# Interleaved rotary embedding on one core: the fp32 tail of the last row is tied to a later store

## The chip, the core and the metric

The kernel runs on one core of one Trainium2 chip. The metric is the device time of one execution in microseconds (us). Before the change it is 316.97 us, the median of three runs (316.95 to 317.14).

## What is computed

The input `x` has 8 batches (called rows here, 0 to 7) of 2048 positions, 16 heads and 64 elements, in fp32: 8.39 MB for each row. Neighbouring elements form pairs, and every pair is rotated by the angle of its position:

```python
x1, x2 = x_pairs[..., 0], x_pairs[..., 1]
out1 = x1 * cos - x2 * sin
out2 = x1 * sin + x2 * cos
out  = np.stack([out1, out2], axis=-1)     # fp32, interleaved again
```

`cos` and `sin` are 2048 x 32 in fp32 and are shared by rows and heads.

## The kernel before

**Layout.** The 2048 positions of a row are laid over 128 partitions, K = 16 positions in each. So a partition holds 16 x 1024 elements of a row, which are 64 KB of contiguous fp32 in memory and 32 KB of bf16 on the chip. The buffer `rows_sb` has NX = 5 slots of one row each, in bf16. Row b lives in slot b % 5: rows 5, 6 and 7 reuse slots 0, 1 and 2.

**Transfers.** `load` and `store` (lines 54 to 63) are DMAs issued by GpSimd (POOL). They convert between fp32 in memory and bf16 in `rows_sb` on the way, and they all go through one queue, called software_dynamic in the profile. A pair of rows goes in one DMA (lines 56 and 63), a single row or part of one in another (lines 54 and 61). Two pieces go another way, as plain fp32 DMAs issued by SyncE (SP), through the queue called hardware_dynamic: the first HEAD = 4 positions of each partition of row 0 (line 90, "the head"), which ScalarE (ACT) converts to bf16 at line 99, and the last TAIL = 4 positions of each partition of row 7 ("the tail"), which ACT converts to fp32 at line 131 and SP stores at line 132. Each of them is 2048 KB of fp32.

**Work.** `rotate` does three VectorE (DVE) operations for each row: the row times the signed sines into `qt` (line 79), the row times the cosines in place (line 80), and the sum with the pair-swapped `qt` (line 85).

**Order.** The schedule is written by hand (`tc.manual_schedule()`), so each engine runs its instructions in the order of the code. The waits between engines are put in from the tiles that instructions share: an instruction that writes a part of a tile waits for earlier readers and writers of that part, DMAs included. The kernel uses this for ordering alone at lines 112 and 130: a copy of a single element writes into a slot, and so has to wait for whatever still reads it.

The end of the order is what the change touches:

```python
store(3, 2)                    # L63: rows 3, 4 from slots 3, 4
rotate(5); rotate(6)
store(5, 2)                    # L63: rows 5, 6 from slots 0, 1
rotate(7)
store(7, k1=K - TAIL)          # L61: first 12 positions of row 7
...
nc.scalar.copy(out=rows_sb[:1, 4, 0, :1], in_=last[:1, K - 1, :1])   # L130
nc.scalar.copy(out=tail, in_=last[:, K - TAIL :])                    # L131
nc.sync.dma_start(out=out_t[:, B - 1, K - TAIL :], in_=tail)         # L132
```

(The three lines with `rotate` and `store` are set closer together here than in the file.) Line 130 reads row 7 and writes one element of slot 4, so it waits for the last rotation and for the store of rows 3 and 4. Lines 131 and 132 come behind it, on ACT and on SP. After the last instruction there is the closing sequence of the program, which the trace lists under line 158: SP waits for every DMA, and the engines meet at a barrier.

Of the kernel before, what the change touches and what calls it, by code (L numbers as in the profile page):

```python
# [2 lines left out]

# [4 lines left out]


@with_exitstack  # L10
def kernel(
    ctx: ExitStack,
    tc: tile.TileContext,
    x: bass.AP,
    cos: bass.AP,
    sin: bass.AP,
    out: bass.AP,
):
    nc = tc.nc
    fp32 = mybir.dt.float32  # L20
    bf16 = mybir.dt.bfloat16
    mult = mybir.AluOpType.mult
    add = mybir.AluOpType.add

    B, S, H, D = x.shape
    P = 128
    K = S // P
    D2 = D // 2
    HD = H * D
    NX = 5  # L30
    HEAD = 4
    TAIL = 4
    REST = 2

    x_t = x.rearrange("b (p k) h d -> p b k (h d)", p=P, k=K)
    out_t = out.rearrange("b (p k) h d -> p b k (h d)", p=P, k=K)
    cos_t = cos.rearrange("(p k) c -> p (k c)", p=P, k=K)
    sin_t = sin.rearrange("(p k) c -> p (k c)", p=P, k=K)

    consts = ctx.enter_context(tc.tile_pool(name="consts", bufs=1))  # L40
    stage = ctx.enter_context(tc.tile_pool(name="stage", bufs=1))

    cos_sb = consts.tile([P, K * D2], fp32)
    sin_sb = consts.tile([P, K * D2], fp32)
    c_tab = consts.tile([P, K, D], bf16)
    s_tab = consts.tile([P, K, D], bf16)
    mark = consts.tile([1, 1], bf16)

    rows_sb = consts.tile([P, NX, K, HD], bf16)

    def load(b, n=1, k0=0, k1=K):
        s = b % NX
        if n == 1:
            nc.gpsimd.dma_start(out=rows_sb[:, s, k0:k1], in_=x_t[:, b, k0:k1])  # L54
        else:
            nc.gpsimd.dma_start(out=rows_sb[:, s : s + n], in_=x_t[:, b : b + n])  # L56

    def store(b, n=1, k1=K):
        s = b % NX
        if n == 1:  # L60
            nc.gpsimd.dma_start(out=out_t[:, b, :k1], in_=rows_sb[:, s, :k1])  # L61
        else:
            nc.gpsimd.dma_start(out=out_t[:, b : b + n], in_=rows_sb[:, s : s + n])  # L63

    def rotate(b, k0=0, k1=K):

        nk = k1 - k0
        xp = rows_sb[:, b % NX, k0:k1]
        qt = stage.tile([P, K, HD], bf16, name="qt", tag="work")

        def rows(a):
            return a.rearrange("p k (h e) -> p k h e", h=H, e=D)

        def tab(a):
            return dataclasses.replace(
                a, offset=a.offset + k0 * D, ap=[a.ap[0], [D, nk], [0, H], [1, D]]
            )

        nc.vector.tensor_tensor(out=rows(qt[:, :nk]), in0=rows(xp), in1=tab(s_tab), op=mult)  # L79
        nc.vector.tensor_tensor(out=rows(xp), in0=rows(xp), in1=tab(c_tab), op=mult)  # L80
        q_swap = dataclasses.replace(
            qt, offset=qt.offset + 1, ap=[qt.ap[0], [2, nk * HD // 2], [-1, 2]]
        )
        x3 = xp.rearrange("p k (a j) -> p (k a) j", j=2)
        nc.vector.tensor_tensor(out=x3, in0=x3, in1=q_swap, op=add)  # L85
        return qt

    with tc.manual_schedule():
        head = stage.tile([P, HEAD, HD], fp32, name="st", tag="work")
        nc.sync.dma_start(out=head, in_=x_t[:, 0, :HEAD])  # L90
        load(0, k0=HEAD)
        nc.gpsimd.dma_start(out=cos_sb, in_=cos_t)  # L92
        nc.gpsimd.dma_start(out=sin_sb, in_=sin_t)  # L93
        load(1, 2)
        load(3)
        load(4, k1=K - REST)
        load(4, k0=K - REST)

        nc.scalar.copy(out=rows_sb[:, 0, :HEAD], in_=head)  # L99
        s2 = s_tab.rearrange("p k (i j) -> p (k i) j", j=2)  # L100
        nc.vector.tensor_copy(out=s2[:, :, 0], in_=sin_sb)  # L101
        nc.vector.tensor_scalar_mul(s2[:, :, 1], sin_sb, -1.0)  # L102
        nc.vector.tensor_copy(  # L103
            out=c_tab.rearrange("p k (i j) -> p (k i) j", j=2),
            in_=cos_sb.to_broadcast([P, K * D2, 2]),
        )
        rotate(0, 0, HEAD)
        rotate(0, HEAD, K)
        rotate(1)

        nc.scalar.copy(out=mark, in_=rows_sb[:1, 4, K - REST - 1, :1])  # L111
        nc.scalar.copy(out=rows_sb[:1, 0, 0, :1], in_=rows_sb[:1, 0, 0, :1])  # L112
        store(0, 2)
        rotate(2)
        store(2)
        load(5, 2)
        load(7)
        rotate(3)
        rotate(4)
        store(3, 2)  # L120
        rotate(5)
        rotate(6)
        store(5, 2)
        rotate(7)
        store(7, k1=K - TAIL)


        tail = stage.tile([P, TAIL, HD], fp32, name="st", tag="work")
        last = rows_sb[:, 7 % NX]
        nc.scalar.copy(out=rows_sb[:1, 4, 0, :1], in_=last[:1, K - 1, :1])  # L130
        nc.scalar.copy(out=tail, in_=last[:, K - TAIL :])  # L131
        nc.sync.dma_start(out=out_t[:, B - 1, K - TAIL :], in_=tail)  # L132


# [1 line left out]
_INS = ['x', 'cos', 'sin']  # L136
_OUTS = [((8, 2048, 16, 64), 'float32')]


# [23 lines left out]
```

## Time and profile before

| what | value |
|---|---|
| median of three runs | 316.97 us (316.95 to 317.14) |
| the profiled execution | 317.52 us |
| its span, first to last instruction | 315.7 us |
| DVE busy | 210.3 us (67%) |
| ACT busy / POOL busy | 8.9 us / 8.9 us |
| share of software_dynamic (POOL's queue) of 16 DMA engines' span | 96.6% |
| share of hardware_dynamic (SP's queue) | 5.7% |
| read from / written to HBM | 67.63 MB / 67.11 MB |

The profiled execution is 0.55 us above the median, and 1.8 us of its time lie outside the span. A DMA is cut into packets that 16 DMA engines work on. Here a packet is one partition's piece of a row. The trace records start, length, size and queue of each packet. For the store of a whole row every DMA engine has eight packets of 64 KB, and for the tail eight packets of 16 KB. At the end of each DMA every engine has one further packet of 4 bytes, its signal. A DMA has landed once all sixteen signals are in. All times below are on the scale of the page, from the start of the span.

### The profile page before, as it was taken

How to read it: one execution, taken by the hardware profiler on the slowest of the kernel's cores; microseconds unless marked ns; L12 is line 12 of the kernel's file. 1: busy time of each engine (PE TensorE's matmuls, PEld its weight loads, DVE VectorE, ACT ScalarE, POOL GpSimd, SP SyncE). 2: the span in 40 equal slices, each digit the busy share in tenths (PEclk: the TensorE clock that was granted, in tenths of full speed). 3: DMA queues.
4: the chain of work that ended last, by engine and by line, in shares of the span. 5: the costliest groups of instructions: out<-in, count | busy, mean ns of one | idle time of the engine just before them, and what ended most of it. 6: DMA issues, size and time to landing. Idle time of an engine off the chain costs nothing.

```text
span 315.7 us, 117 instructions
## 1 busy us (share of the span) xinstructions
DVE 210.3 (67%) x30; ACT 8.9 (3%) x6; POOL 8.9 (3%) x18
## 2 busy tenths in 40 slices
DVE  0009995099999999999992000899999999900000
ACT  1030000000000000000000000000000000040000
POOL 5000000000000000000000000000000000000000
DMA  8999999999999999999999999999999999999997
GB/s 260 254 282 199 199 199 266 199 199 220 220 232 257 399 531 399 399 498 432 399 199 253 212 199 199 266 199 332 440 490 399 399 506 423 399 399 465 459 372 299
DMA packets 2816, 102.24 MB, mean 324 GB/s; under 512 B 256, under 2 KB 256, under 8 KB 512
## 3 DMA queue, kind: packets, MB, share of 16 engines
q0 software_dynamic: 2528, 98.04, 96.6%
q1 hardware_dynamic: 288, 4.19, 5.7%
HBM read 67.63 MB, written 67.11 MB: 427 GB/s over the span
## 4 chain that ended last, share of the span: by engine, by line
DVE 66%; another core or an unknown queue 13%; ACTq 1%; issue 0%; ACT 0%; DVEq 0%
DVE rows_sb L80 22%; DVE rows_sb L85 22%; DVE qt L79 22%; ACTq L158 1%; DVE c_tab L103 0%; ACT rows_sb L130 0%; DVEq L79 0%; DVEq L80 0%
## 5 line engine op out<-in xcount | busy, mean ns | idle before, releaser
L79 DVE TENSOR_TENSOR qt<-rows_sb,s_tab 128x16384 bf16<-128x16384 bf16 (+2 forms) x9 | 69.7, 7743 | 42.0 <-DMA rows_sb<-in_x_dram 41.8
L80 DVE TENSOR_TENSOR rows_sb<-rows_sb,c_tab 128x16384 bf16<-128x16384 bf16 (+2 forms) x9 | 69.7, 7743 | 0.4
L85 DVE TENSOR_TENSOR rows_sb<-rows_sb,qt 128x16384 bf16<-128x16384 bf16 (+2 forms) x9 | 69.7, 7744 | 0.3
L101 DVE CAST s_tab<-sin_sb 128x512 bf16<-128x512 f32 x1 | 0.5, 454 | 23.8 <-DMA sin_sb<-in_sin_dram 23.8
L63 POOL DMA_DIRECT2D out_dram<-rows_sb x3 | 2.2, 719 | 184.0 <-ACT rows_sb L112 94.3
L130 ACT COPY rows_sb<-rows_sb 1x1 bf16<-1x1 bf16 x1 | 0.2, 194 | 177.5 <-DVE rows_sb L85 177.5
L99 ACT CAST rows_sb<-st 128x4096 bf16<-128x4096 f32 x1 | 3.6, 3604 | 13.2 <-DMA st<-in_x_dram 13.2
L131 ACT CAST st<-rows_sb 128x4096 f32<-128x4096 bf16 x1 | 3.6, 3598 | 0.0
L54 POOL DMA_DIRECT2D rows_sb<-in_x_dram x5 | 2.9, 605 | 19.1 <-DMA out_dram<-rows_sb 18.3
L111 ACT COPY mark<-rows_sb 1x1 bf16<-1x1 bf16 x1 | 0.2, 193 | 80.3 <-DMA rows_sb<-in_x_dram 80.3
L61 POOL DMA_DIRECT2D out_dram<-rows_sb x2 | 1.1, 556 | 40.4 <-DVE rows_sb L85 40.4
L56 POOL DMA_DIRECT2D rows_sb<-in_x_dram x2 | 1.5, 728 | 25.0 <-DMA out_dram<-rows_sb 25.0
L99 ACT ACT_TABLE_LOAD x1 | 1.3, 1283 | 0.7 <-PEq L147 0.7
L103 DVE CAST c_tab<-cos_sb 128x1024 bf16<-128x1024 f32 x1 | 0.7, 685 | 0.0
L93 POOL DMA_DIRECT2D sin_sb<-in_sin_dram x1 | 0.6, 562 | 0.0
L92 POOL DMA_DIRECT2D cos_sb<-in_cos_dram x1 | 0.6, 554 | 0.0
L102 DVE TENSOR_SCALAR s_tab<-sin_sb 128x512 bf16<-128x512 f32 x1 | 0.4, 444 | 0.0
L112 ACT COPY rows_sb<-rows_sb 1x1 bf16<-1x1 bf16 x1 | 0.2, 188 | 0.0
L147 POOL MEMSET const-float32-0.0<- 128x1 f32 x1 | 0.1, 99 | 0.2 <-issue 0.2
L147 POOL MEMSET const-bfloat16-1.0<- 128x1 bf16 x1 | 0.1, 103 | 0.0
L147 POOL MEMSET const-float32-1.0<- 128x1 f32 x1 | 0.1, 99 | 0.0
L147 POOL MEMSET const-uint8-127<- 128x1 uint8 x1 | 0.1, 99 | 0.0
## 6 DMA issues: line engine op xcount, KB each, us to landing
rows_sb<-in_x_dram POOLq DMA_DIRECT2D x2, 8192.0 KB, 58.5
rows_sb<-in_x_dram POOLq DMA_DIRECT2D x2, 4096.0 KB, 68.0
out_dram<-rows_sb POOLq DMA_DIRECT2D x1, 6144.0 KB, 37.3
rows_sb<-in_x_dram POOLq DMA_DIRECT2D x1, 3584.0 KB, 94.8
rows_sb<-in_x_dram POOLq DMA_DIRECT2D x1, 3072.0 KB, 21.2
st<-in_x_dram SPq DMA_DIRECT2D x1, 2048.0 KB, 14.4
out_dram<-st SPq DMA_DIRECT2D x1, 2048.0 KB, 33.7
rows_sb<-in_x_dram POOLq DMA_DIRECT2D x1, 512.0 KB, 96.8
```

What stands on the lines that cost most here:

```text
L54: nc.gpsimd.dma_start(out=rows_sb[:, s, k0:k1], in_=x_t[:, b, k0:k1])
L56: nc.gpsimd.dma_start(out=rows_sb[:, s : s + n], in_=x_t[:, b : b + n])
L61: nc.gpsimd.dma_start(out=out_t[:, b, :k1], in_=rows_sb[:, s, :k1])
L63: nc.gpsimd.dma_start(out=out_t[:, b : b + n], in_=rows_sb[:, s : s + n])
L79: nc.vector.tensor_tensor(out=rows(qt[:, :nk]), in0=rows(xp), in1=tab(s_tab), op=mult)
L80: nc.vector.tensor_tensor(out=rows(xp), in0=rows(xp), in1=tab(c_tab), op=mult)
L85: nc.vector.tensor_tensor(out=x3, in0=x3, in1=q_swap, op=add)
L92: nc.gpsimd.dma_start(out=cos_sb, in_=cos_t)
L99: nc.scalar.copy(out=rows_sb[:, 0, :HEAD], in_=head)
L103: nc.vector.tensor_copy(out=c_tab.rearrange("p k (i j) -> p (k i) j", j=2), in_=cos_sb.to_broadcast([P, K * D2, 2]),)
L131: nc.scalar.copy(out=tail, in_=last[:, K - TAIL :])
L158: with _tile.TileContext(nc) as tc:
```

## The change

The one-element copy at line 130 writes into slot 6 % 5 = 1 instead of slot 4. Slot 1 holds row 6, which is read by the store of rows 5 and 6. So line 130 now waits for that store (and for the last rotation, as before), and lines 131 and 132 come behind it. Nothing else changes: every engine has the same instructions in the same order. The waits of line 130 grow from three semaphores to five.

```diff
         tail = stage.tile([P, TAIL, HD], fp32, name="st", tag="work")
         last = rows_sb[:, 7 % NX]
-        nc.scalar.copy(out=rows_sb[:1, 4, 0, :1], in_=last[:1, K - 1, :1])
+        nc.scalar.copy(out=rows_sb[:1, 6 % NX, 0, :1], in_=last[:1, K - 1, :1])
         nc.scalar.copy(out=tail, in_=last[:, K - TAIL :])
         nc.sync.dma_start(out=out_t[:, B - 1, K - TAIL :], in_=tail)
```

## The prediction

> **What bounds the kernel now.** I read the page's slices and queues first, then its DMA issues.
>
> ```profile
> DVE  0009995099999999999992000899999999900000
> DMA  8999999999999999999999999999999999999997
> q0 software_dynamic: 2528, 98.04, 96.6%
> q1 hardware_dynamic: 288, 4.19, 5.7%
> out_dram<-rows_sb POOLq DMA_DIRECT2D x1, 6144.0 KB, 37.3
> out_dram<-st SPq DMA_DIRECT2D x1, 2048.0 KB, 33.7
> ```
>
> The DMA engines are busy from end to end, and DVE is idle in the last five slices. The bound is the DMA engines. The last two rows are the store of row 7 and the tail. From the timeline of the last part:
>
> ```profile
> 250.95 0.72 POOL L63 DMA_DIRECT2D out_dram<-rows_sb  x1 [82.44 <-DVE rows_sb L85]
> ...
> 276.86 0.19 ACT L130 COPY rows_sb<-rows_sb 1x1 bf16<-1x1 bf16 x1 [177.48 <-DVE rows_sb L85]
> 276.96 3.60 ACT L131 CAST st<-rows_sb 128x4096 f32<-128x4096 bf16 x1
> 277.13 0.54 POOL L61 DMA_DIRECT2D out_dram<-rows_sb  x1 [25.46 <-DVE rows_sb L85]
> 280.58 0.35 SPq L132 DMA_DIRECT2D out_dram<-st  x1
> ```
>
> Line 130 was released by the last rotation (L85). Its other wait, for the store of rows 3 and 4, was over by 256.2, when the last signal of that DMA came. So the old tie delays nothing. Adding the page's time to landing to the issue, row 7 lands at 277.13 + 37.3 = 314.43 and the tail at 280.58 + 33.7 = 314.28. Next, the DMA traffic between 286.7 and 296.3, and then the window table (stretch, length, busy DVE, ACT and POOL, clock, DMA share, GB/s):
>
> ```profile
> DMA packets 112, 4.19 MB, mean 437 GB/s; under 512 B 0, under 2 KB 0, under 8 KB 0
> q0 software_dynamic: 48, 3.15, 76.0%
> q1 hardware_dynamic: 64, 1.05, 26.8%
> ```
>
> ```profile
> 277.00:286.70 9.70, 0.00 (x0) 3.56 (x2) 0.54 (x1) 1.00 1.01 432
> 287.00:296.00 9.00, 0.00 (x0) 0.00 (x0) 0.00 (x0) 1.00 1.02 435
> 297.00:304.00 7.00, 0.00 (x0) 0.00 (x0) 0.00 (x0) 1.00 1.04 442
> 306.20:313.40 7.20, 0.00 (x0) 0.00 (x0) 0.00 (x0) 1.00 2.04 437
> ```
>
> In the first and last stretch data move only on POOL's queue, in the two between both queues take turns packet by packet. The rate is 432 to 442 GB/s either way. (The share of 2.04 in the last counts waiting signal packets as busy.) Last, the closing sequence, as the trace lists line 158, and SP's wait in it:
>
> ```profile
> L158 SPq EVENT_SEMAPHORE  x8: 17/28/28, 297.3 to 315.7; - x8
> L158 POOLq DRAIN  x3: 45/82/37927, 277.1 to 315.5; - x3
> ...
> SPq L158 <- DMA out_dram<-rows_sb: 33.4, 2, 17.1
> ```
>
> SP takes the DMAs in a fixed order: that of rows 5 and 6 (297.3), that of row 7 (314.43), four others that were over long ago, and last the tail. A POOL drain ends at 277.1 + 37.93 = 315.03.
>
> **Part 1: when the tail starts.** A 64 KB row takes 2.41 us on each DMA engine when POOL's queue runs alone (packet starts 279.55, 281.96, 284.37) and 3.03 us beside a tail packet (287.42, 290.45, 293.48). A tail packet costs 0.62 us. Four of them stood ahead of the landing of rows 5 and 6 at 297.30 (64 packets on q1 over 16 engines). The new wait puts them behind it, so that store lands at 297.30 - 4 x 0.62 = 294.8. ACT and SP need from 276.86 to 280.58, 3.72 us, and a further wait instruction some 0.05 us: SP issues the tail at about 298.6, 18 us later than now. Nothing is queued behind line 130 on ACT but line 131, and nothing behind line 132 on SP but the closing waits. POOL has issued the store of row 7 at 277.13 and waits for neither, DVE is done.
>
> **Part 2: where the DMA engines end.** With no tail before it, the store of row 7 starts at 294.1 on the first engine. Its eight 48 KB packets take 1.81 us each when alone (306.21, 308.02, 309.83, 311.64), so POOL's queue alone lasts until 308.5. The tail reaches the engines between 1.0 us after its issue (the head: issue 0.74, first packet 1.74) and 6.2 us (the tail before: 280.58 to 286.78, behind packets already taken in), so between 299.6 and 304.8. That is 3.7 to 8.9 us before POOL's queue is empty, and this is the cover of the 18 us delay: no engine goes idle, the same packets come in another order. If the tail were issued after 307.5, every further us would cost one. The end is 308.5 + 8 x 0.62 = 313.48 on the first engine, where it is 313.44 now, and 0.41 us later on the last one. Between three and eight tail packets now run alone at the very end. Alone such a packet took 0.61 us after the store of rows 5 and 6 (296.52 to 297.13), and in the head 0.62 us. Change of part 2: +0.04 us, from -0.1 to +0.2.
>
> **Part 3: the closing sequence.** Now row 7 signals last, the final signal arriving 0.56 us after its packet starts (313.85 to 314.41). SP sees it at 314.43 and steps through the remaining waits until 314.67, where it checks the tail. Afterwards row 7 signals first and those steps are done while the tail still runs. The tail's last signal packet starts at about 313.9 and arrives 0.34 to 0.43 us later (0.34 for the head, 0.43 for the store of rows 3 and 4): 314.25 to 314.35. SP passes its last wait at about 314.3 instead of 314.67, so 0.35 us earlier. Then POOL's drain: it ended at 315.03, 0.23 us after SP had reported at 314.80 and 0.62 us after row 7 had landed. No POOL instruction runs from 277.67 on, so I read it as waiting for POOL's own DMAs. If so, it will end some two us earlier, and the barrier opens 0.05 us after SP's report at 314.45: 314.50 instead of 315.07, a gain of 0.57 us. If it follows SP instead, only the 0.35 us. I take 0.5, nearer to the drain that waits for its DMAs.
>
> **Sum.** The profiled span ends 0.04 - 0.5, about 0.46 us earlier: 317.52 becomes 317.06 us, and the median of 316.97, which is 0.55 below the profiled execution, becomes 316.5.
>
> **One wait weighed.** The sixteen signal packets of the tail, started at 306.21 on the first engine, took 7.28 us each, against 22 ns for those of the head. On each engine they end with the signal of row 7: 306.21 + 7.28 = 313.49, and 313.44 + 0.05. I read this as a wait for the other queue's writes. [...] The trace agrees in the end times, but shows no SP store that ends alone.
>
> **Rivals.** (a) *The close shortens by more than I count.* If the drain goes, the landing delay falls to the head's 0.34 us, and the tail's packets at the end run at 0.61, the gain is 0.57 + 0.05 + 0.08 = 0.7: 316.3, to 316.1. For it: a drain of 37.93 us. Against: each piece is at its best end. (b) *The tail's signal has its own delay*, the case slower than before. If the 7.28 us belong to an SP store into memory and not to the other queue, they follow the last data and nothing hides them: tail done near 313.9 + 7.3 = 321.2, time 316.97 + 321.2 - 314.3 = 323.9. It decides from a signal wait of about 1.6 us, where the gain of the close is used up and 0.64 us are lost. For it: the only SP store in the trace shows this wait. Against: it ends to 0.05 us with the signal of row 7. (c) *Lone tail packets run slower.* The first packets of the head took 0.89 to 1.40 us; at 1.1 for five packets the loss is 5 x 0.48 = 2.4 us, less 0.5: 318.9. Against: the head's following packets and the lone tail packet at 0.61 to 0.62. (d) *Nothing moves*: the close keeps its length, since its pace is set by the drain and that by something else. 316.97 + 0.04 = 317.0. That the new tie does nothing is out: its store lands 18 us after the last rotation.
>
> **Chances.** A measurement of this kernel tells about 0.2% from no change, which is 0.63 us: 316.34 to 317.60 is no difference. My forecast (316.4 to 316.8) has 0.55, (d) 0.15, (a) 0.20, (b) 0.05, (c) 0.05. So faster 0.20, same 0.70, slower 0.10. The range takes in (a), the forecast and (d) with the 0.2 us of part 2: 316.1 to 317.3. It leaves out (b) and (c).
>
> **What would show it.** In the profile afterwards: SP's DMA of line 132 at 298.6; line 130 released by a DMA near 294.8; the first packet on SP's queue between 299.6 and 304.8; a GB/s line that stays near 435 until 313.9; tail signal packets with lengths far below 7 us; the tail landing at 314.3 and row 7 one to three us before it; POOL's drain ending before 314.5. Wrong would be: an idle stretch on the DMA engines after 308.5, lone tail packets well above 0.62 us, or a tail signal that waits.

## The result, and the profile after

The median fell from 316.98 us (22 runs) to 316.35 us (22 runs): 0.63 us less, ratio 0.9981, 95% interval 0.9975 to 0.9986. The forecast was 316.5 us, with 316.1 to 317.3 as its range. The gain lies at the very edge of what the prediction called no difference, and 0.05 us under the band that it called its own forecast (316.4 to 316.8).

The lines of the page after that answer to those shown before: slices and queues, then the last two DMAs with their us to landing.

```profile
DVE  0009995099999999999992000899999999910000
DMA  8999999999999999999999999999999999999997
q0 software_dynamic: 2528, 98.04, 96.8%
q1 hardware_dynamic: 288, 4.19, 3.4%
out_dram<-rows_sb POOLq DMA_DIRECT2D x1, 6144.0 KB, 34.0
out_dram<-st SPq DMA_DIRECT2D x1, 2048.0 KB, 15.5
```

The DMA engines are as full as before. The share of SP's queue fell from 5.7% to 3.4%, which is the waiting of its signal packets that has gone (7.28 us on each engine, 2.3% of the span, are now 9 ns). The timeline after:

```profile
276.48 0.55 POOL L61 DMA_DIRECT2D out_dram<-rows_sb  x1 [25.46 <-DVE rows_sb L85]
294.25 0.19 ACT L130 COPY rows_sb<-rows_sb 1x1 bf16<-1x1 bf16 x1 [195.42 <-DMA out_dram<-rows_sb]
294.35 3.60 ACT L131 CAST st<-rows_sb 128x4096 f32<-128x4096 bf16 x1
297.97 0.35 SPq L132 DMA_DIRECT2D out_dram<-st  x1
```

Line 130 is now released by a DMA, and SP issues the tail at 297.97 instead of 280.58. Row 7 lands at 276.48 + 34.0 = 310.5 and the tail at 297.97 + 15.5 = 313.5: the order of the two has turned round. Next, the closing sequence (line 158). The first of SP's drains comes 0.04 us behind its last wait, and the second one, 0.055 us later, is SP's report to the barrier (times of the report are its start). The barrier opens with the first of the four POOL semaphore instructions. Here are the lines of the kernel before:

```profile
L158 POOLq EVENT_SEMAPHORE  x4: 17/17/17, 315.1 to 315.6; - x4
L158 SPq DRAIN  x3: 7/7/7, 314.7 to 315.3; - x3
```

And of the changed kernel:

```profile
L158 SPq EVENT_SEMAPHORE  x8: 17/28/28, 298.4 to 314.3; - x8
L158 POOLq EVENT_SEMAPHORE  x4: 17/17/17, 313.7 to 314.2; - x4
L158 POOLq DRAIN  x3: 45/90/34653, 276.5 to 314.1; - x3
L158 SPq DRAIN  x3: 7/7/7, 313.6 to 313.9; - x3
```

Last, what SP waited for in it (us in total, times, longest us):

```profile
SPq L158 <- DMA out_dram<-rows_sb: 12.1, 1, 12.1
SPq L158 <- DMA out_dram<-st: 2.8, 1, 2.8
```

The last that SP waits for is now the tail, for 2.8 us. POOL's long drain ended at 276.454 + 34.653 = 311.11, well before that, and the barrier opened at 313.67, 0.03 us after SP's report at 313.64. Before, the drain ended at 315.03, after SP's report at 314.79, and the barrier opened at 315.07.

The profiled executions differ by more than the medians: 317.52 and 316.12 us. Of these 1.40 us, 0.69 were there when the store of rows 3 and 4 signalled (last signal packet at 255.813 before, 255.127 after), ahead of anything the change touches. This is a spread between executions: a kernel with the new tie, the last experiment below, has that packet at 255.91. So I count from it. From that packet to the end of the span it is 59.925 us before and 59.223 us after. The 0.70 us between them fall into three parts:

| us | before | after | difference |
|---|---|---|---|
| from that packet to the last signal packet of all | 58.04 | 58.03 | -0.01 |
| from the last signal packet to the last landing | 0.56 | 0.35 | -0.21 |
| from the last landing to the end of the span | 1.33 | 0.85 | -0.48 |

The DMA engines need the same time. The gain is in what follows them.

### The profile page after: what moved, and what is told of

Its sections match the earlier page's. It is cut to its first block, busy times and chain, and to the rows that moved or that the text cites. A ratio compares the mean times of both kernels' runs of the same rounds, so it can differ in the third digit from the quotient of the medians.

```text
span 314.4 us, 118 instructions
## 1 busy us (share of the span) xinstructions
DVE 210.3 (67%) x30; ACT 8.9 (3%) x6; POOL 8.9 (3%) x18
## 4 chain that ended last, share of the span: by engine, by line
DVE 42%; issue 17%; DMA 14%; another core or an unknown queue 13%; ACTq 1%; POOL 0%; ACT 0%; DVEq 0%; POOLq 0%
DMA out_dram<-rows_sb 14%; DVE rows_sb L80 14%; DVE rows_sb L85 14%; DVE qt L79 14%; ACTq L158 1%; POOL out_dram L63 0%; DVE c_tab L103 0%; ACT rows_sb L130 0%; ACTq L130 0%; DVEq L80 0%; DVEq L79 0%; POOLq L63 0%; POOLq L61 0%
## 6 DMA issues: line engine op xcount, KB each, us to landing
out_dram<-st SPq DMA_DIRECT2D x1, 2048.0 KB, 15.5
```

## The experiments

Three theories stood against each other. *Closing*: the gain is the closing sequence, which is short when SP's DMA lands last and long when POOL's does, because a POOL drain follows POOL's last landing. *Order*: the DMA engines work faster when the tail keeps out of the store of rows 5 and 6. *Signal*: the tail's waiting signal packets hold up the landing of row 7. The kernels move the time of the tail with either tie, by converting it several times in a row, leave the tail out, or shrink it.

**The new tie again** (no edit to the changed kernel).

> The changed kernel once more, beside the others. Closing theory (the gain is the closing sequence: with the tail landing last, SP's other waits and POOL's drain are over by then): about 0.6 us less than the kernel before, ratio 0.998; last landing to end of span 0.85 us instead of 1.33. Order theory (the DMA engines move the same bytes faster once the tail is out of the way of the store of rows 5 and 6): the same ratio, but the time from the landing signals of rows 3 and 4 to the last signal packet would be shorter by about 0.5 us or more.

Measured: 316.31 us, ratio 0.9978 (0.9969 to 0.9988). 58.03 us from the signals of rows 3 and 4 to the last signal packet, landing 0.35 us after it, close 0.84 us. The gain repeats, and no part of it is in the first of the three figures. That is against the order theory.

**The old tie, tail converted twice.**

```diff
         nc.scalar.copy(out=rows_sb[:1, 4, 0, :1], in_=last[:1, K - 1, :1])
         nc.scalar.copy(out=tail, in_=last[:, K - TAIL :])
+        nc.scalar.copy(out=tail, in_=last[:, K - TAIL :])
```

> The old tie, with the tail converted twice in a row at line 131: the tail is issued about 3.6 us later than before (near 284.1), so its first packet comes near 290 and one tail packet fewer or two fewer stand ahead of the landing of rows 5 and 6. The tail's packets are still done before row 7's. Closing theory: row 7 still lands last, POOL's drain still ends 0.62 us after that, no gain, ratio 1.000 (316.9 to 317.1). Order theory: a quarter to a half of the gain, 0.15 to 0.3 us, ratio 0.999. Signal theory (row 7's landing is held up by the tail's waiting signals, 0.56 us instead of 0.35): no gain, as the tail's signals still wait.

Measured: 317.14 us, ratio 1.0 (0.9992 to 1.0009). Only two tail packets for each engine now started before the store of rows 5 and 6 signalled, and nothing was gained. Row 7 landed last at 314.04, the tail at 313.88, and the close took 1.33 us. From its closing sequence (line 159 in this kernel):

```profile
L159 POOLq DRAIN  x3: 45/82/37997, 276.7 to 315.1; - x3
L159 SPq DRAIN  x3: 7/7/7, 314.4 to 314.9; - x3
```

The long drain ends at 276.66 + 38.00 = 314.66, 0.62 us after row 7 had landed and 0.24 us after SP's report at 314.42. The signal packets of the tail waited 3.66 us.

**The old tie, tail converted five times** (the same edit with four lines).

> The old tie, with the tail converted five times in a row: issued about 14.4 us later than before, near 295, without waiting for any store. First packet near 301.3, some four packets of row 7 left, so the tail ends last. Closing theory: the full gain although the tie is the old one, ratio 0.998 (316.3 to 316.5), POOL's drain over well before SP's report. Order theory: the full gain too, since no tail packet stands before rows 5 and 6 have landed. If the wait itself mattered and not the time of the tail, there would be no gain: 1.000.

Measured: 316.27 us, ratio 0.9972 (0.9961 to 0.9983). The timeline, with the line numbers of this kernel, shows that no store is waited for:

```profile
276.35 0.19 ACT L130 COPY rows_sb<-rows_sb 1x1 bf16<-1x1 bf16 x1 [177.44 <-DVE rows_sb L85]
...
290.98 3.60 ACT L135 CAST st<-rows_sb 128x4096 f32<-128x4096 bf16 x1
294.61 0.35 SPq L136 DMA_DIRECT2D out_dram<-st  x1
```

The tail was issued late and landed last, at 313.66, and the close took 0.84 us. So the gain doesn't need the new wait, only the tail's time.

**No tail: row 7 whole by POOL.**

```diff
-        store(7, k1=K - TAIL)
-        tail = stage.tile([P, TAIL, HD], fp32, name="st", tag="work")
...
-        nc.sync.dma_start(out=out_t[:, B - 1, K - TAIL :], in_=tail)
+        store(7)
```

> No SP tail: row 7 is stored whole by POOL, and lines 130 to 132 are left out, so its last four positions go through the same converting store as the others. The bytes written are the same. Closing theory: POOL's DMA lands last, the drain ends 0.62 us after it and SP's steps 0.39 us after it, so the close has its old length of about 1.3 us: 316.9 to 317.1, ratio 1.000, or 0.2 us less if the landing takes 0.4 us without the tail's waiting signals. Order theory: no tail packet mixes with anything, the DMA engines end as early as with the new tie or earlier: the gain is kept, ratio 0.998 or less. Signal theory: row 7 lands 0.2 us earlier after its signal packet than before, a third of the gain, ratio 0.9993.

Measured: 316.71 us, ratio 0.9994 (0.9984 to 1.0003). Here nothing mixes with anything, and yet more than half of the gain is missing: the median is 0.36 us above that of the changed kernel. The data took 57.93 us (0.11 less than with a tail), the landing 0.43 us after the last signal packet, the close 1.34 us. Its closing sequence:

```profile
L151 POOLq DRAIN  x3: 45/96/37638, 276.5 to 314.6; - x3
L151 SPq DRAIN  x3: 7/7/7, 313.8 to 314.4; - x3
```

The drain ends at 276.50 + 37.64 = 314.14, 0.62 us after the landing at 313.52; SP had reported at 313.84. The long close is back, with POOL's DMA landing last. The 0.13 us by which row 7 lands sooner than before (0.43 against 0.56) are what the signal theory asked for, but they come from one execution each.

**The new tie, tail converted three times.**

> The new tie, with the tail converted three times in a row: issued near 305.2 instead of 298. Cover theory (the delay costs nothing as long as packets of row 7 are left): POOL's packets last to about 308 without a tail, so the DMA engines have no gap, first tail packet between 306 and 308, and the end stays where the new tie has it: 316.2 to 316.4, ratio 0.998. Rival (the delay already costs, because a late tail has most of its eight packets alone at the end and its first one comes 6 to 7 us after the issue): first packet at 311.5, a gap of some 3.5 us, 319.8, ratio 1.009.

Measured: 316.34 us, ratio 0.9979 (0.997 to 0.9987). SP issued the tail at 305.50. POOL's queue gave its last signal packets from 308.18 on, the first tail packet started at 308.18 too, and all eight ran alone, 0.61 to 0.64 us apart. A delay of another 7.5 us cost nothing.

**The new tie, tail converted five times.**

> The new tie, with the tail converted five times in a row: issued near 312.4, past the point of 307.5 from which the prediction lets every us cost one. Cover theory: row 7 lands near 308.4, the engines stand idle until 313.4, then eight packets of 0.61 us, last landing near 319.0, close 0.85: 321.5 (321 to 322), ratio 1.014 to 1.016. If the start of an SP store took 6.2 us whatever stands before it: first packet near 318.6, 326.7, ratio 1.031.

Measured: 321.53 us, ratio 1.0141 (1.0127 to 1.0155). The window table (stretch, length, busy DVE, ACT and POOL, clock, DMA share, GB/s):

```profile
306.00:308.00 2.00, 0.00 (x0) 2.00 (x1) 0.00 (x0) 1.00 0.92 393
308.90:313.10 4.20, 0.00 (x0) 3.62 (x2) 0.00 (x0) 1.00 0.00 0
313.60:319.00 5.40, 0.00 (x0) 0.00 (x0) 0.00 (x0) 1.00 0.80 340
```

The DMA engines stand idle (0 GB/s) between row 7 and the tail. The cover of the delay is used up about where the prediction put it: the tail was issued at 312.58, which is 5.1 us past 307.5 (5.7 us, if one counts that this execution was 0.6 us ahead of the one before the change at the store of rows 3 and 4), and the median is 5.2 us above that of the changed kernel. On idle engines its first packet came 0.84 us after the issue.

**The old tie, tail converted three times.**

> The old tie, with the tail converted three times in a row: issued near 287.4, first packet at about 294 just as row 7 starts, so the two DMAs have eight packets each left and end together. Closing theory: the barrier opens at the later of POOL's landing + 0.66 and the tail's report, so the gain depends on which is last: none (1.000) if POOL's signals come last, 0.2 to 0.5 us (0.9985 to 0.9994) if the tail is last by one packet of 0.6 us. Order theory is out by the first runs (58.03 us from the signals of rows 3 and 4 to the last signal packet, in the old and the new tie alike).

Measured: 317.09 us, ratio 1.0002 (0.9993 to 1.0011). The first tail packet started at 293.50. One tail packet came before the signal of rows 5 and 6 and a second one before row 7's first packet at 294.75, so on the first engine the tail's data were done at 309.3 and those of row 7 at 312.9. POOL's signals came last (landing 313.81, tail 313.63), the close took 1.33 us, no gain. The tail's signal packets, started at 311.12, waited 1.85 us.

**The new tie, TAIL = 1.**

```diff
-    TAIL = 4
+    TAIL = 1
```

> The new tie with TAIL = 1: SP stores one position of each partition instead of four (8 packets of 4 KB for each DMA engine, some 0.16 us each), POOL the other fifteen. The bytes are the same. Closing theory: the gain depends on which DMA lands last, not on how large it is, so a quarter of the tail keeps it: 316.1 to 316.4, ratio 0.9975 to 0.9985. If the gain grew with the tail's size, a quarter of it would be left: 316.8, ratio 0.9995.

Measured: 316.44 us, ratio 0.998 (0.9971 to 0.9989). A quarter of the tail keeps the gain. Here row 7 landed at 313.86 and the tail at 314.31, so drain and SP report come together:

```profile
L158 POOLq DRAIN  x3: 45/90/37292, 277.2 to 314.9; - x3
L158 SPq DRAIN  x3: 7/7/7, 314.4 to 314.7; - x3
```

The drain ends at 277.184 + 37.292 = 314.48, again 0.62 us after row 7; SP reports at 314.45; the barrier opens at 314.52. The close took 0.88 us.

Side by side, the five kernels in which the tail lands last and the data have no gap (the changed kernel and its repeat, old tie with five conversions, new tie with three, TAIL = 1) close in 0.84 to 0.88 us and land 0.35 us after their last signal packet. The four in which POOL lands last close in 1.33 to 1.34 us and land 0.43 to 0.63 us after it. In all ten profiled executions the drain ended 0.62 us after POOL's own last landing, whenever that was (308.69 to 314.41), and the barrier opened 0.03 to 0.05 us after the later of two times, the end of this drain and SP's report. From there to the end of the span it took 0.67 to 0.68 us each time. So the 0.48 us of the close are accounted for.

## Why the prediction was right

**The bound and the old tie** held. The old wait was over long before the last rotation (256.24 us against 276.86 in the kernel before), and the new one decides (294.25, forecast 294.8; the whole execution ran 0.69 us earlier).

**When the tail starts** held for the issue (297.97, forecast 298.6, and 298.66 with the 0.69 us added). The first packet at 304.34 lies between the forecast 299.6 and 304.8, but only because the execution ran early: it came 6.37 us after the issue, where the prediction had 6.2 us as the most. Nothing hung on it, since row 7 still had packets left.

**Where the DMA engines end** held: forecast 0.04 us later, measured 0.01 us earlier. In the kernel with three conversions a further delay of 7.5 us, with packets of row 7 still left at the issue, cost nothing (316.34 us). The single kernel past that point, with five conversions, lost about as much as it was late: 5.2 us, issued 5.1 to 5.7 us past the prediction's 307.5.

**The closing sequence** had the right mechanism, and its size came out too small: 0.46 us forecast, 0.70 us in the profiles, 0.63 us in the medians. The prediction took 0.5 us, between 0.35 (the drain follows SP) and 0.57 (the drain waits for POOL's own DMAs). The experiments settle this choice: the drain ended 0.62 us after POOL's last landing in all ten executions, whenever SP reported, so 0.57 was the end to take. A further 0.04 us is a slip in the sum: the 314.50 of part 3 starts from 313.9, which already has the later end of part 2 in it, and the sum takes off these 0.04 us once more. The rest is in the landing of the tail. Its last signal packet came 0.06 us earlier than 313.9 (313.15, with 0.69 added), and its signal took 0.35 us, where the prediction's 314.3 allows about 0.40.

**The signal wait** is settled in its size: the tail's signals waited 7.28, 3.66 and 1.85 us as its last data came nearer to the end of row 7, ended with row 7's signals each time (in the kernel before both at 313.49 on the first engine), and took 9 ns in the six kernels where the tail was last. This fits the prediction's reading, a wait for the other queue's writes, for which the trace before had only the end times of a single SP store. The traces now show SP stores that end alone, without a wait. What exactly a signal waits for, they leave open: in the kernel before, the signal packet started at 306.21 and ended only behind three packets of row 7 that started after it (308.02, 309.83 and 311.64 on the first engine).

**The rivals.** (a), a larger gain from the close, is nearest: 0.70 us in the traces, with all pieces near their best end, and a median of 316.35 us between its 316.3 and the lower end of the forecast's own band, 316.4. So the range and the mechanism held, and the size was nearer to that of a rival with a chance of 0.20. (b), a delay of the tail's own signal, and (c), slow lone packets, are out: 9 ns, and 0.61 to 0.64 us for each of eight lone packets. (d), nothing moves, is out by the interval.

**What stays open** is a part of the landing, which gave 0.21 us. In the three kernels in which tail signals waited, row 7 landed 0.56 to 0.63 us after its last signal packet, and 0.16 to 0.18 us after the tail. In the seven others it landed 0.36 to 0.43 us after that packet, and the tail, where it came last, 0.35 us after its own. This fits the signal theory, but no experiment took only the waiting signals away, so this cause is argued and not shown.

No kernel here beats the changed one clearly: 316.27 to 316.44 us is one level.

## What to carry to other kernels

With the DMA engines full to the end, it mattered here which queue's DMA landed last: a POOL drain ended 0.62 us after POOL's last landing in all ten executions, and a last piece that went through SP hid it (a close of 0.84 to 0.88 us instead of 1.33 to 1.34). A last piece of a quarter of the size was enough in the kernel with TAIL = 1, where POOL's DMA landed 0.46 us ahead of it and drain and SP's report came together (314.48 and 314.45). Its issue could be delayed to 305.50 us at no cost, with packets left in the other queue, and in the one kernel that issued it after that queue had run dry (312.58, which is 5.1 to 5.7 us past the prediction's 307.5) the median was 5.2 us higher. Read such a change from a common event shortly ahead of it: up to that event these ten kernels do the same work, and it still came between 255.13 and 255.91, which is more than the change brought after it.

## What was not expected

A late issue took effect later here than its own time suggests. The first tail packet came 0.84 us after the issue on idle DMA engines, but 6.2 to 7.5 us after it in the kernels where POOL's queue was full (before, after and five experiments), with two to three of POOL's packets of 48 to 64 KB started on each engine in between. That those packets had been taken in already, as the prediction has it, is a reading of the packet times that no run tested by itself.
